# First layer's MLP: plain products replaced by seven half-size products for eight, with the context tokens apart

## The chip, the cores and the metric

One core of one Trainium2 chip runs the whole program. The metric is the device time of one launch in microseconds (us); before the change it is 2879.24 us, the median of 3 runs (2877.9 to 2879.73).

## What is computed

The reference is a two-layer backbone over 1024 latent tokens and 256 context tokens of width 1024. Layer 0 (even) mixes by latent attention and a chunked gate, layer 1 (odd) by gated linear attention. Every layer modulates its RMS norm with vectors that come from the conditioning (six vectors per layer, each a 1024x1024 product with one vector), and closes with a squared-ReLU MLP of hidden width 4096:

```python
def sqrelu_mlp(h, w1, w2):
    return jnp.square(jax.nn.relu(h @ w1)) @ w2

xl = xl + ml[5] * sqrelu_mlp(modulate(rmsnorm(xl, norm2_g[i]), ml[3], ml[4]), mlp_w1[i], mlp_w2[i])
if need_ctx:   # layer 0 only
    xc = xc + mc[5] * sqrelu_mlp(modulate(rmsnorm(xc, norm2_g[i]), mc[3], mc[4]), mlp_w1[i], mlp_w2[i])
```

So layer 0's MLP serves 1280 tokens, layer 1's only the 1024 latent ones. Everything is float32.

## The kernel before, in words

**Products.** Tokens lie along the free dimension in three parts, `TCS`: latent 0 (512), latent 1 (512) and context (256), called 0, 1 and 2 here as in the code. TensorE multiplies float32 by splitting each operand into a rounded part and the rest ("hi" and "lo"): `mm3` (lines 204 to 206) issues hi·hi, hi·lo and lo·hi, three matmuls for one 128x128 weight block and one part of tokens. The hi of a weight is a cast on ScalarE (line 165), its lo a subtraction on VectorE (line 171). A weight block of 1024 columns is loaded through the pool `raws` (3 buffers) and split by `load_w`; `Weights.take(depth)` hands out the next one and first fills the queue up to `depth` blocks ahead. Almost all other tiles share the pool `slots`, 43 buffers of 4 KB per partition.

**Layer 0's MLP** is `mlp` (lines 1096 to 1170). For each of 16 pairs of hidden blocks it takes two blocks of w1, multiplies them with the parts in the order `O3`, makes relu squared and its split, takes two blocks of w2, multiplies and adds into x at once (line 1154). The first pair goes through `first_gemm`, which applies the norm chunk by chunk. Beside it, the generator `bg` makes layer 1's modulation vectors with `ada`: for each of 48 weight tiles of 512 KB a dot product with the conditioning, for the first 16 tiles also with the context's vector. One dot product is a multiplication on GpSimd and a summing activation on ScalarE (`ada_dot`, lines 318 and 319), the other one multiply-and-sum on VectorE (`ada_reduce`, line 332).

**Layer 1's MLP** is `FastMlp` (lines 1173 to 1673). It treats the two latent halves and the halves of the weights as a 2x2 product and needs seven half-size products for eight (the steps A11, A12, S2, S1, S3, S4, A22 of `STEPS`). Its right operands (names 11, 21, 22 and T1 to T4, four tiles each) come from the modulated norm by `scaled`, `shifted`, `half` and `combine`. In `first` (lines 1476 to 1515) one step is 12 matmuls of 512 columns; a pair of hidden blocks has seven steps. Around the products, each step prepares a weight operand three steps ahead (`prepare`: cast on ScalarE, subtraction on VectorE), and `took` handles the result of the step before. A `Hidden` that is "light" squares with two activations on ScalarE (lines 1297, 1298); one that is not does it on VectorE (line 1302). The first two pairs (`PLAIN`) of layer 1 are plain, the next two (`EARLY`) partly, the other 12 take all seven steps. The second product runs over 28 jobs of four groups of 12 matmuls each.

**What sets the order.** Outside `FastMlp.run` a scheduler orders each engine's instructions by the order of their emission and by what is ready. Inside `FastMlp.run` (`manual_schedule`, lines 1570 to 1576) each of the five queues takes its instructions strictly in the order in which the code emits them, so an instruction that waits holds all behind it on its engine. `half` emits, for one chunk,

```python
self.scaled(0, k)                                   # VectorE, line 1210
nc.scalar.activation(hi, t, AF.Identity, bias=b)    # ScalarE, line 1217
nc.vector.scalar_tensor_tensor(lo, t, b, f(hi), op0=ALU.add, op1=ALU.subtract)   # VectorE, line 1218
```

and `apply_norm` (lines 273 to 288) the same three with lines 276, 277, 280. `combine` and `prepare` go through `FastMlp.split`, which emits the cast, then the pending subtraction of the call before. `Norm.begin` is four small matmuls, a VectorE step, a power on GpSimd and a VectorE step (lines 233 to 237); `Norm.end` is a matmul (line 246).

**Around it.** `out_proj` before the MLP ends with the blocks of its last two output chunks part by part in the order `O3`, and begins and ends the norm of a part behind the blocks of the next. `odd_proj` after it starts with `first_gemm` on two weight blocks.

## Time and profile before

| | |
|---|---|
| median of 3 runs | 2879.24 us (2877.9 to 2879.73) |
| profiled execution's own time | 2879.53 us |
| its span, first to last instruction | 2877.7 us |
| TensorE busy | 2755.9 us (96%), mean granted clock 0.983 |
| VectorE, ScalarE, GpSimd busy | 1945.6, 1221.7 and 668.0 us |
| first matmul to last of layer 0's MLP | 780.3 to 1675.2 us |

Times in views are microseconds from the span's start unless marked ns. Matmuls are pipelined: the duration of one is longer than the distance between the starts of two, and the work of a stretch is counted with that distance. PE is TensorE, PEld its weight load, DVE VectorE, ACT ScalarE, POOL GpSimd, SP SyncE. A wait is put down to the engine whose signal came last.

### The profile page before, as it was taken

What the parts mean: (1) busy time and instruction counts of PE and PEld (TensorE: products, weight loads), DVE (VectorE), ACT (ScalarE), POOL (GpSimd) and SP (SyncE); (2) the same over time, 40 slices, a digit from 0 to 9 for tenths busy, and PEclk for the clock granted to TensorE, in tenths of its full rate; (3) what the DMA queues carried; (4) which work ended last, traced back from release to release, by engine and by line L of the source; (5) the groups of instructions that cost most, each with busy time, mean ns of one, the idle gap of its engine ahead of it and who ended that gap; (6) DMA issues with size and microseconds to landing.
All of it is one profiled execution on the core that took longest, in us unless ns stands there. A gap on an engine that the chain in (4) does not pass through costs nothing.

```text
span 2877.7 us, 38606 instructions
## 1 busy us (share of the span) xinstructions
PE 2755.9 (96%) x14752; PEld 2364.8 (82%) x14752; DVE 1945.6 (68%) x3271; ACT 1221.7 (42%) x2375; POOL 668.0 (23%) x608
## 2 busy tenths in 40 slices
PE   5999999999799999999999999999899999999997
PEld 3887899888688888888888878997788788888885
DVE  7848788886778745544544571544774867788887
ACT  4534677774333233222212241876452533344342
POOL 4335455532432332210000010114620111100000
PEclk9999999999899999999999999999999999999998
DMA  6232000026223232321111121335254444483431
GB/s 242 70 115 71 13 13 17 15 88 214 81 74 95 96 103 88 96 73 37 51 31 37 54 74 52 110 112 182 102 198 146 182 159 143 160 302 138 154 135 64
DMA packets 109914, 301.11 MB, mean 105 GB/s; under 512 B 10816, under 2 KB 24256, under 8 KB 109728
## 3 DMA queue, kind: packets, MB, share of 16 engines
q1 hardware_dynamic: 93232, 242.00, 24.9%
q0 software_dynamic: 16496, 56.63, 5.4%
q8 instruction: 116, 1.90, 0.3%
q14 instruction: 70, 0.57, 0.1%
HBM read 229.39 MB, written 69.21 MB: 104 GB/s over the span
## 4 chain that ended last, share of the span: by engine, by line
PE 76%; DVE 9%; issue 6%; ACT 3%; POOL 3%; DMA 3%; SPq 0%; POOLq 0%; DVEq 0%; ACTq 0%
PE b L204 22%; PE b L206 22%; PE b L205 22%; PE b L883 2%; PE b L868 2%; DVE adaj L332 1%; PE b L458 1%; POOL adaj L318 1%; DVE wlo L171 1%; DMA ada<-in_adaT 1%; PE b L1819 1%; DVE h L280 1%; DVE acc L225 1%; DMA hr<-hsp 1%; PE b L1775 1%
## 5 line engine op out<-in xcount | busy, mean ns | idle before, releaser
L204 PE MATMUL b<-h,whi 128*128 128x512 f32 (+1 forms) x1544 | 563.3, 367 | 3.7 <-ACT h L277 1.8
L206 PE MATMUL b<-h,wlo 128*128 128x512 f32 (+1 forms) x1544 | 560.7, 363 | 4.9 <-DVE wlo L171 4.8
L205 PE MATMUL b<-h,whi 128*128 128x512 f32 (+1 forms) x1544 | 561.8, 364 | 3.4 <-DVE h L280 2.2
L205 PEld LDWEIGHTS b<-h,whi 128*128 128x128 f32 x1544 | 294.0, 190 | 52.0 <-DVE h L171 3.2
L206 PEld LDWEIGHTS b<-h,wlo 128*128 128x128 f32 x1544 | 293.6, 190 | 52.0 <-DVE wlo L171 6.9
L204 PEld LDWEIGHTS b<-h,whi 128*128 128x128 f32 x1544 | 293.3, 190 | 51.2 <-ACT h L165 3.2
L205 PE MATMUL b<-B,W 128*128 128x512 f32 (+1 forms) x840 | 325.8, 388 | 5.6 <-DVE B L1566 5.6
L204 PE MATMUL b<-B,W 128*128 128x512 f32 (+1 forms) x840 | 325.9, 388 | 3.6 <-DVE u L1331 3.1
L1154 DVE SCALAR_TENSOR_TENSOR x<-b,mod,x 128x512 f32<-128x512 f32 (+1 forms) x384 | 248.5, 659 | 117.4 <-PE b L206 115.1
L206 PE MATMUL b<-B,W 128*128 128x512 f32 (+1 forms) x840 | 325.2, 387 | 0.0
L318 POOL TENSOR_TENSOR adaj<-ada,sc 128x1024 f32<-128x1024 f32 x80 | 220.6, 2774 | 381.4 <-PE b L206 184.3
L204 PE MATMUL b<-hid,whi 128*128 128x512 f32 (+1 forms) x768 | 272.8, 355 | 0.0
L205 PE MATMUL b<-hid,whi 128*128 128x512 f32 (+1 forms) x768 | 272.0, 354 | 0.0
L206 PE MATMUL b<-hid,wlo 128*128 128x512 f32 (+1 forms) x768 | 271.9, 354 | 0.0
L1123 DVE TENSOR_TENSOR relu<-relu 128x512 f32<-128x512 f32 (+1 forms) x96 | 79.6, 835 | 193.8 <-ACT relu L1116 193.8
L319 ACT ACTIVATE adaj<-adaj 128x1024 f32<-128x1024 f32 x80 | 84.8, 1061 | 294.0 <-POOL adaj L318 294.0
L205 PEld LDWEIGHTS b<-B,W 128*128 128x128 f32 x840 | 159.3, 190 | 39.6 <-DVE B L1566 7.7
L204 PEld LDWEIGHTS b<-B,W 128*128 128x128 f32 x840 | 159.3, 190 | 36.9 <-ACT W L165 3.1
L206 PEld LDWEIGHTS b<-B,W 128*128 128x128 f32 x840 | 159.2, 189 | 31.2
L171 DVE TENSOR_TENSOR wlo<-raw,whi 128x1024 fp32r<-128x1024 f32 x120 | 153.0, 1281 | 45.2 <-ACT whi L165 43.6
L204 PEld LDWEIGHTS b<-hid,whi 128*128 128x128 f32 x768 | 145.5, 189 | 20.5 <-issue 0.2
L205 PEld LDWEIGHTS b<-hid,whi 128*128 128x128 f32 x768 | 145.4, 189 | 20.3 <-issue 0.2
(288 smaller groups left out, 5690.9 us busy)
## 6 DMA issues: line engine op xcount, KB each, us to landing
raw<-in_w SPq DMA_DIRECT2D x130, 512.0 KB, 4.2
ada<-in_adaT SPq DMA_DIRECT2D x96, 512.0 KB, 4.2
hr<-hsp SPq DMA_DIRECT2D x56, 512.0 KB, 4.1
hsp<-hid POOLq DMA_DIRECT2D x48, 512.0 KB, 4.8
raw<-in_od_win SPq DMA_DIRECT2D x25, 512.0 KB, 3.7
x<-in_xT SPq DMA_DIRECT2D x20, 512.0 KB, 8.4
xsp<-x SPq DMA_DIRECT2D x16, 512.0 KB, 3.8
x<-xsp SPq DMA_DIRECT2D x16, 512.0 KB, 10.4
```

What stands on the lines that cost most here:

```text
L171: (lo or nc.vector).tensor_sub(dst[1], src, f(dst[0]))
L204: nc.tensor.matmul(ps, lhsT=ah, rhs=bh, start=start, stop=False, skip_group_check=more)
L205: nc.tensor.matmul(ps, lhsT=ah, rhs=bl, start=False, stop=False, skip_group_check=more)
L206: nc.tensor.matmul(ps, lhsT=al, rhs=bh, start=False, stop=stop, skip_group_check=more)
L225: (add or nc.vector).tensor_add(acc, acc, sq)
L280: nc.vector.scalar_tensor_tensor(dst[1], t, b[:, d:d + 1], f(dst[0]), op0=ALU.add, op1=ALU.subtract)
L318: nc.gpsimd.tensor_mul(j, t, sc[w])
L319: nc.scalar.activation(j, j, AF.Copy, accum_out=mod(l, part, w)[:, d:d + 1])
L868: nc.tensor.transpose(tb[:, a, b], p[:, o:o + P], ident)
L883: nc.tensor.matmul(av, lhsT=V[self.kts[2 * g + a]][:, h], rhs=self.pts[g][:, a, s], start=(g == 0 and a == 0 and s == 0), stop=(g == ng - ...
L1123: nc.vector.tensor_mul(r, r, r)
L1154: nc.vector.scalar_tensor_tensor(x, ps, gate[i][:, d:d + 1], x, op0=ALU.mult, op1=ALU.add)
```

## The change

Layer 0's MLP is made by `FastMlp` as well, now with all 16 pairs taking seven steps (`plain` and `early` are 0), all light. The context tokens don't fit into that scheme: `context_in` multiplies them with all 32 blocks of w1 in front and stores the hidden values in memory, `context_out` multiplies these with all of w2 behind; both load and split the weights a second time for it. `context_in` makes the right operands of the latent products beside its blocks, two steps of `operands` per block; `context_out` begins the next layer's norm and applies it for the latent parts. Layer 1's modulation vectors are made by `ada_paced`, both dot products on VectorE, one tile at every odd step of `first`, the tile loaded two steps ahead into `raws`. `O3` puts the context first. Layer 1's own MLP keeps its parameters.

```diff
+    csp = dr.tile([NFF, P, 256], F32, name="csp", tag="csp")
+    cxsp = dr.tile([ND, P, 256], F32, name="cxsp", tag="cxsp")
...
+    def load_halves(src):
+        raw = raws.tile([P, 2, 512], F32, name=nm("raw"), tag="raw")
+        nc.sync.dma_start(raw, src.rearrange("b p c -> p b c"))
+        return split_w(raw.rearrange("p b c -> p (b c)"))
...
+    def ada_paced(items):
+        for l, part, which in items:
+            for d in range(ND):
+                t = raws.tile([P, D], F32, name=nm("ada"), tag="raw")
+                nc.sync.dma_start(t, adaT[l, part * ND + d])
+                yield
+                for w in which:
+                    j = t if w == which[-1] else slot([D], n="adaj")
+                    nc.vector.tensor_tensor_reduce(j, t, sc[w], scale=1.0, scalar=0.0, op0=ALU.mult, op1=ALU.add,
+                                                   accum_out=mod(l, part, w)[:, d:d + 1])
+                t = None
+            for w in which:
+                ada_end(l, part, w)
...
                     elif pace:
-                        while (0, k) not in on_chip:
+                        while (order[0], k) not in on_chip:
                             run(load, 1)
...
-    def mlp(l, norm, order, gate, bg, ab, parts=None, done=None):
...
-        def __init__(self, l):
-            self.l = l
+        def __init__(self, l, plain, early, bg=iter(())):
+            self.l, self.plain, self.early, self.bg = l, plain, early, bg
...
-            nc.gpsimd.dma_start(bsp[k], f(self.made_last))
+            if self.plain:
+                nc.gpsimd.dma_start(bsp[k], f(self.made_last))
...
-            early = p < EARLY
+            early = p < self.early
-                self.hids[p] = self.Hidden(p, early)
+                self.hids[p] = self.Hidden(p, early or not self.early)
...
             NP = self.NP
-            steps = [(p, c) for p in range(PLAIN, NP) for c, _, _ in STEPS
-                     if p >= EARLY or c in ("S1", "S2", "S3", "S4", "A22")]
+            steps = [(p, c) for p in range(self.plain, NP) for c, _, _ in STEPS
+                     if p >= self.early or c in ("S1", "S2", "S3", "S4", "A22")]
             todo, n = [], 0
-            for p in range(PLAIN, NP):
+            for p in range(self.plain, NP):
                 mine = [c for q, c in steps if q == p]
-                if p == EARLY:
+                if p == self.early and p:
                     for c in ("11", "21"):
                         todo.append((n - 7, lambda c=c: self.again(c)))
-                if p > PLAIN:
+                if p == 0:
+                    todo += [(k - 3.5, lambda c=c: self.prepare(0, c)) for k, c in enumerate(mine) if k > 2]
+                elif p > self.plain:
                     todo.append((n - 8, lambda p=p: self.load_pair(p)))
...
+            self.late = None
...
                 self.product(held[o], self.ops.pop((p, c)), b, new)
+                if n % 2:
+                    run(self.bg, 1)
                 if last:
...
-        def run(self, gate, parts, done):
+        def run(self, *args):
-            out = self.all(gate, parts, done)
+            out = self.all(*args)
-        def all(self, gate, parts, done):
+        def operands(self):
+            for k in range(8):
+                self.half(k)
+                yield
+            self.spill(0)
+            for j in range(4):
+                self.scaled(1, j)
+                self.scaled(1, j + 4)
+                yield
+                self.shifted("22", j + 4)
+                self.combine("T1", j)
+                yield
+            self.spill(1)
+            self.norm.xs = self.xs = None
+            for c in ("T2", "T3", "T4"):
+                for j in range(4):
+                    self.combine(c, j)
+                    if c == "T3":
+                        del self.ts[1, j]
+                    yield
+            self.load_pair(0)
+            yield
+            self.flush()
+            for c in ("S1", "S2", "S3", "S4"):
+                self.add_up(0, c)
+                yield
+            for c in ("A11", "A12", "S2"):
+                self.prepare(0, c)
+                yield
+        def context_in(self):
+            norm = self.norm
+            self.late, self.T = None, {}
+            for j, t in enumerate(norm.xs[2].tiles):
+                nc.sync.dma_start(cxsp[4 * j:4 * j + 4].rearrange("d p t -> p d t"), t)
+            self.xs = norm.xs
+            b = norm.ab[0][1]
+            self.db = small(4, n="db")
+            nc.vector.tensor_sub(self.db, b[:, 4:8], b[:, 0:4])
+            ops = self.operands()
+            late = None
+            def act(b, ps):
+                r = tmp([256], n="r")
+                nc.scalar.activation(r, ps, AF.Relu)
+                if b % 4 == 0:
+                    self.c = slot([4, 256], n="hc")
+                nc.scalar.activation(self.c[:, b % 4], r, AF.Square)
+                if b % 4 == 3:
+                    nc.gpsimd.dma_start(csp[b - 3:b + 1].rearrange("b p t -> p b t"), self.c)
+                    self.c = None
+            for b in range(NFF):
+                w = W.take(min(2, NFF - 1 - b))
+                ps = bank([512])[:, :256]
+                gemm(ps, w, norm.hs[2])
+                w = None
+                if b < 2:
+                    (norm.end if b else norm.begin)(1)
+                run(ops, 2)
+                if late:
+                    late()
+                late = lambda b=b, ps=ps: act(b, ps)
+            run(ops)
+            late()
+            self.flush()
+            norm.hs[2] = None
+        def context_out(self, gate, after, x):
+            after.xs[2] = x
+            self.c = self.t = None
+            def fetch(b):
+                t = slot([4, 256], n="hc")
+                nc.sync.dma_start(t, csp[b:b + 4].rearrange("b p t -> p b t"))
+                return t
+            def made(b):
+                if b % 4 == 0:
+                    self.t = self.u
+                if b % 4 == 2:
+                    self.u = fetch((b + 2) % NFF)
+                if b % 2 == 0:
+                    self.c = slot([2, 2, 256], F32R, n="B")
+                o = self.c[:, b % 2, 0], self.c[:, b % 2, 1]
+                split(o, self.t[:, b % 4])
+                return o
+            self.u = fetch(0)
+            h = made(0)
+            n = 0
+            for m in range(2):
+                pss = [bank([512])[:, :256] for _ in range(4)]
+                for b in range(NFF):
+                    if b % 2 == 0:
+                        w = W.take(min(2, (NFF - 2 - b) // 2 + (1 - m) * NFF // 2))
+                    cs = (b % 2) * 512
+                    for g in range(4):
+                        ds = slice(cs + g * P, cs + (g + 1) * P)
+                        mm3(pss[g], (w[0][:, ds], w[1][:, ds]), h, b == 0, b == NFF - 1)
+                    if n in (2, 4, 6, 8):
+                        (after.end if n % 4 == 0 else after.begin)((n - 2) // 4)
+                    if b % 2:
+                        w = None
+                    n += 1
+                    if n < 2 * NFF:
+                        h = made(b + 1 if b + 1 < NFF else 0)
+                    if n >= 10 and n % 4 == 0:
+                        for i in range(2):
+                            after.apply(i, min((n - 8) // 4, ND))
+                for g in range(4):
+                    d = 4 * m + g
+                    nc.vector.scalar_tensor_tensor(x[d], pss[g], gate[2][:, d:d + 1], x[d], op0=ALU.mult, op1=ALU.add)
+                    after.accs[2] = sumsq(after.accs[2], x[d], 256)
+            self.c = self.t = self.u = None
+            return after
+        def all(self, gate, parts, done, ab=None):
-            self.begin()
+            if self.plain:
+                self.begin()
+            else:
+                self.context_in()
...
-            accs = [None] * len(parts)
-            after = Norm([[x[:, q[1]:q[2]] for x in xs[q[0]]] for q in parts], accs,
-                         [(0, q[2] - q[1]) for q in parts], self.norm.ab)
+            if self.plain:
+                accs = [None] * len(parts)
+                after = Norm([[x[:, q[1]:q[2]] for x in xs[q[0]]] for q in parts], accs,
+                             [(0, q[2] - q[1]) for q in parts], self.norm.ab)
+            else:
+                accs = [None] * 3
+                after = Norm(xs + [None], accs, TCS, ab)
...
-                cuts = [(0, 256), (256, 512)] if last else [(0, 512)]
+                cuts = [(0, 256), (256, 512)] if last and done else [(0, 512)]
...
-                        if last:
+                        if last and done:
...
+            if not self.plain:
+                self.context_out(gate, after, load_x(cxsp, 0, 256))
...
-    O3, O2 = (0, 2, 1), (0, 1)
+    O3, O2 = (2, 0, 1), (0, 1)
-    ff = lambda l: [lambda l=l, c=c, j=j, w=w: load_w(w[l, c * 2 + j])
-                    for c in range(NFF // 2) for w in (w1, w2) for j in range(2)]
-    W.add(*[lambda d=d: load_w(ev_wout[d]) for d in range(ND)], *ff(0))
+    W.add(*[lambda d=d: load_w(ev_wout[d]) for d in range(ND)])
+    W.add(*[lambda b=b: load_w(w1[0, b]) for b in range(NFF)])
+    W.add(*[lambda b=b, m=m: load_halves(w2[0, b:b + 2, :, m * 512:m * 512 + 512])
+            for m in range(2) for b in range(0, NFF, 2)])
...
-    bg = chain(*(ada(1, p, (0, 1) if p < 2 else (0,)) for p in range(6)))
-    norm = mlp(0, norm, O3, both(0, 5), bg, mods2(1, 0))
-    pre = odd_proj(norm, O3)
+    fast = FastMlp(0, 0, 0, ada_paced([(1, p, (0, 1) if p < 2 else (0,)) for p in range(6)]))
+    fast.norm = norm
+    norm = fast.run(both(0, 5), [(0, 0, 512), (1, 0, 512)], None, mods2(1, 0))
+    pre = odd_proj(norm, (0, 1, 2))
-    fast = FastMlp(1)
+    fast = FastMlp(1, PLAIN, EARLY)
```

## Rows read from the trace of the kernel before

**Rows 1.** The page's first part: busy time, share of the span, instructions.
```profile
PE 2755.9 (96%) x14752; PEld 2364.8 (82%) x14752; DVE 1945.6 (68%) x3271; ACT 1221.7 (42%) x2375; POOL 668.0 (23%) x608
```

**Rows 2.** Windows: stretch, its length, busy time by engine (instructions), clock, DMA share, GB/s.
```profile
780.30:1675.20 894.90, 889.55 (x4634) 766.03 (x4633) 522.55 (x743) 239.74 (x399) 147.89 (x61) 1.00 0.22 70
1675.20:1700.00 24.80, 23.02 (x125) 19.05 (x124) 23.10 (x43) 13.15 (x24) 4.29 (x3) 1.00 0.18 64
2321.00:2521.00 200.00, 200.00 (x884) 165.62 (x883) 148.66 (x232) 62.32 (x115) 27.23 (x40) 1.00 0.43 152
2560.00:2790.00 230.00, 229.84 (x1014) 190.02 (x1013) 195.07 (x306) 95.90 (x173) 0.00 (x0) 1.00 0.43 153
```

**Rows 3.** Timeline of PE, layer 0's MLP: 23 matmuls of 512 columns, 24 of 256.
```profile
899.78 0.39 PE L205 MATMUL b<-h,whi 128*128 128x512 f32 x1
...
904.99 0.28 PE L204 MATMUL b<-h,whi 128*128 128x256 f32 x1
...
907.87 0.40 PE L204 MATMUL b<-h,whi 128*128 128x512 f32 x1
```

**Rows 4.** Timeline of ACT and DVE, layer 1: weight split, then four `scaled`.
```profile
2238.97 1.03 ACT L165 CAST whi<-raw 128x1024 fp32r<-128x1024 f32 x1
2240.03 1.23 DVE L171 TENSOR_TENSOR wlo<-raw,whi 128x1024 fp32r<-128x1024 f32 x1 [0.23 <-ACT whi L165]
2241.17 2.72 DVE L1210 SCALAR_TENSOR_TENSOR t<-x,mod,b 128x512 f32<-128x512 f32 x4
```

**Rows 5.** The same view: hi of one chunk; cast and lo of one `combine`.
```profile
2207.58 0.72 ACT L1217 ACTIVATE B<-t,mod 128x512 fp32r<-128x512 f32 x1 [0.70 <-DVE t L1210]
...
2247.18 0.62 ACT L165 CAST B<-T 128x512 fp32r<-128x512 f32 x1 [1.38 <-DVE T L1244]
2247.83 0.69 DVE L1190 TENSOR_TENSOR B<-T,B 128x512 fp32r<-128x512 f32 x1 [0.69 <-ACT B L165]
```

**Rows 6.** Groups by line: engine, operation, count, busy us, mean ns, idle before.
```profile
L165 ACT CAST hid<-relu 128x256 fp32r<-128x256 f32 x32 | 12.8, 404 | 11.0 <-DVE relu L1123 11.0
L171 DVE TENSOR_TENSOR hid<-relu,hid 128x256 fp32r<-128x256 f32 x32 | 13.4, 421 | 9.0 <-ACT hid L165 9.0
```

**Rows 7.** Timeline of DVE: a norm's begin, with the power on POOL between its two steps.
```profile
2188.04 0.16 DVE L235 TENSOR_SCALAR rs<-b 128x4 f32<-128x4 f32 x1
...
2189.32 0.69 DVE L237 TENSOR_TENSOR acc<-ident,rs 128x512 f32<-128x512 f32 x1 [1.05 <-POOL rs L236]
```

**Rows 8.** Timeline of DVE and ACT, layer 1, pair 3, which is light: one square.
```profile
2308.12 0.68 DVE L1294 TENSOR_TENSOR c<-b,u 128x512 f32<-128x512 f32 x1
2310.67 0.69 DVE L1190 TENSOR_TENSOR W<-S,W 128x512 fp32r<-128x512 f32 x1 [1.87 <-ACT W L165]
...
2308.84 0.63 ACT L1297 ACTIVATE c<-c 128x512 f32<-128x512 f32 x1 [1.36 <-DVE c L1294]
...
2310.04 0.60 ACT L165 CAST W<-S 128x512 fp32r<-128x512 f32 x1
```

**Rows 9.** Multiply-and-sum on DVE: one beside quiet POOL, then the group over all.
```profile
755.52 1.21 DVE L332 CUSTOM_DVE_ANT_0 adaj<-ada,sc 128x1024 f32<-128x1024 f32 x1
...
L332 DVE CUSTOM_DVE_ANT_0 adaj<-ada,sc 128x1024 f32<-128x1024 f32 x76 | 132.9, 1766 | 11.7 <-DMA ada<-in_adaT 11.6
```

**Rows 10.** Timeline of PE: end of `out_proj`, then the second product's first job in layer 1.
```profile
760.63 1.86 PE L233 MATMUL b<-ones,acc 128*128 128x1 f32 x8 [16.70 <-DVE acc L225]
766.99 0.41 PE L204 MATMUL b<-h,whi 128*128 128x256 f32 x1
767.20 0.41 PE L205 MATMUL b<-h,whi 128*128 128x256 f32 x1
...
2543.04 0.50 PE L205 MATMUL b<-B,W 128*128 128x512 f32 x1 [1.12 <-DVE B L1566]
```

**Rows 11.** Windows behind that wait; columns as in rows 2.
```profile
760.00:770.00 10.00, 9.37 (x40) 8.51 (x41) 3.07 (x7) 0.83 (x2) 1.04 (x1) 0.59 0.23 79
770.00:780.00 10.00, 10.00 (x48) 8.28 (x47) 5.53 (x10) 3.05 (x5) 0.69 (x1) 1.00 0.00 0
```

71 lines of the change are left out of this document (removed).

## The prediction

> **What bounds the kernel now.** I read the page's shares first: TensorE is busy 96% of the span [rows 1], so time goes only where matmuls go away or where TensorE comes to wait. Then the windows by stage [rows 2]: layer 0's MLP takes 894.9 us and TensorE idles for 5.3 us of it, while layer 1's MLP, already in the seven-product scheme, keeps TensorE as full (200.00 of 200 us in the first product, 229.84 of 230 in the second) with VectorE at 74% and 85%. Then the timeline, for the price of a matmul [rows 3]: 23 of 512 columns start within 5.21 us, 0.2266 us each; 24 of 256 within 2.88 us, 0.120 us each. Last the timelines of VectorE and ScalarE, for the handoffs between the two, since inside `FastMlp.run` every queue is strictly in order.
>
> The faster scheme removes matmuls, but the context's blocks now stand alone at 2.88 us each, and beside them stands work that was spread over 894.9 us. The question is how long that work takes in order.
>
> **Matmuls removed.** Before, per part: 32 blocks x 8 chunks x 3, for w1 and for w2, 1536 matmuls; 1536 x (2 x 0.2266 + 0.120) = 880.5 us. After: latent 16 pairs x 7 steps x 12 and 28 jobs x 48, 2 x 1344 x 0.2266 = 609.1; context 1536 x 0.120 = 184.3, together 793.4. Gain 87.1 us. The stage before has 894.9 - 880.5 = 14.4 us beyond its matmuls (idle, norm matmuls, a low clock at its start), and `odd_proj` idles 1.8 us at its start [rows 2]. All this goes; below stands what comes instead.
>
> **Context in front.** One block in program order: cast of the weight two blocks ahead, its subtraction, the 24 matmuls, two steps of `operands`, relu and square of the block before. ScalarE's next cast stands behind that square, and VectorE's next subtraction behind that cast, so the two engines form one chain per block, and TensorE gets weights at its pace. Prices [rows 4]: cast 1.03, then the subtraction, whose successor starts 1.14 later; four `scaled` take 2.72, so 0.66 from start to start and 0.74 alone; a hi 0.72, a cast of 512 0.62 and a subtraction 0.69 [rows 5], which with the same overlap of 0.08 costs 0.60 to 0.61 where the next is ready; relu and square of 256 some 0.4 each, like the cast of that shape [rows 6].
> - Blocks 1 to 3 hold two `half` each, and in `half` VectorE waits for ScalarE's hi before its lo: 1.05 + 1.14 + (0.75 + 0.72 + 0.66) + (0.75 + 0.66) + 0.7 + handoffs of 0.03 = 6.6 us. Block 0 has `norm.begin` instead of a relu: TensorE's 2.9, four small matmuls, 1.28 to the step behind the power [rows 7], then two halves, 9.1 us.
> - Blocks 4 to 7 (two `scaled`, a hi, a lo, T1): 1.05 + 1.14 + 0.66 + 0.75 + 0.72 + 0.66 + 0.68 + 0.53 + 0.7 + handoffs = 7.0 us.
> - Blocks 8 to 13 (two of T2 to T4, subtraction deferred): 1.05 + 1.14 + 0.66 + 0.60 + 0.75 + 0.53 + 0.7 = 5.5 us.
>
> Sum 9.1 + 19.8 + 28 + 33 = 89.9; 2.2 later block 16 has its weights, and 16 more blocks at 2.88 make 138.2 us against 92.2 of matmuls: **+46**. Lower bound, if the handoffs were hidden: VectorE alone has 1.14 + 2.4 per block, 18 blocks x 0.65 = +11; upper bound +56, if buffers of `slots` run short and each of the 14 blocks pays 0.7 us more for a subtraction. I take the chain, as the queues are in order and rows 5 show VectorE idle for such a cast.
>
> **First product.** Per pair VectorE has seven subtractions, four sums, four differences and three additions, 18 x 0.605 = 10.9 us of 19.03. Being light, each of three squares puts two activations and a cast between an addition and the next subtraction: 1.87 us of waiting [rows 8]; one of the three lies under the sums. 14.7 us, no bound. Now 64 multiply-and-sums come in, two per odd step for the first 16 tiles, one for 32 more. The trace has one at 1.21 us beside a quiet GpSimd, as long as a weight's subtraction, so a successor comes 1.14 later [rows 4]; the mean of all is 1.77 [rows 9]. GpSimd only issues stores here, so 1.14: 2 x 3.5 x 1.14 = 8.0 make 22.7 us per pair, 3.7 over TensorE's, for 32 steps or 4.57 pairs: 17; minus one step's slack at A22 (2.7): **+14.5**. With one per odd step 18.7 us, just covered. Bounds: +5 (the waits overlap) and +60 (price 1.77, below). Between the products TensorE waits 1.1 in layer 1 [rows 10]: **+1.1**.
>
> **Context behind.** Its start: the last residual add, a square, the cast of h and of the first weight (nothing is fetched ahead) and its subtraction, some 4 us, and 1.5 more until the second h: +5.5. Two begins at 2.4 us each of subtraction, power and the lo of the next h, which is made only one block ahead: +4.8, and 2.4 for the norms' matmuls. Then eight times per four blocks (5.76 us) two `apply_norm`, each waiting for its hi: 2 x 2.16, two weight subtractions 2.28, four of 256 some 1.4, and 0.4 until the weight's cast: 8.4 us. 8 x 2.65 less 3 to 4 of lead: +17.5. **+30** in all; bounds +10 and +40. **`odd_proj`** has no weights ready now: two casts and subtractions behind the last squares, **+6**; bounds 1 and 9.
>
> **`out_proj`.** Context first: its last blocks are shorter cover, its norm is cheaper. The wait of 16.70 us for the sum of squares [rows 10] moves with VectorE's backlog and isn't removed. 0; bounds -8 and +5. Modulation off GpSimd and ScalarE: no gain, both have slack; 48 loads of 512 KB on SyncE, 25 MB in 305 us, hide beside 16 MB of weights: 134 GB/s, where layer 1's first product moved 152 without a wait [rows 2]. Each takes the one buffer of `raws` that two pairs of weights leave, and its wait for the release holds the next pair's loads on SyncE's queue; these are due three steps (8.2 us) before they are used, so I add nothing, and a late landing is inside the +60. Stores of context and x: hidden.
>
> **Sum.** -87.1 - 14.4 - 1.8 + 46 + 14.5 + 1.1 + 30 + 6 = -5.7 us. Against the profiled execution's own 2879.53 (span 2877.7, median 2879.24): **2874 us**. The matmul gain is nearly all given back. 0.2% (5.8 us) is about what a measurement of this kernel can tell from no change, so the forecast sits on that edge: 2858 to 2890 with the terms' small errors.
>
> **Clock.** Behind the 16.70 us wait [rows 10] the granted clock is 0.59, partly the lower of the two levels (1.2 and 2.4 GHz), and 1.00 in the ten us after [rows 11]; a matmul of 256 then starts every 0.21 us [rows 10], a block 5.1 us. In front, TensorE idles half of each block, so it may sit at the lower level. That is still below the chain's 5.5 to 7.0 us and costs nothing until block 14; I add nothing.
> The Trainium skill (TensorE: Matmul & The Clock Gate, section "HAM oscillation — how this bites in real kernels") says that waits between bursts put the array back to the lower clock every time, which speaks against blocks apart. The trace agrees that a wait lowers it and shows a quick return.
>
> **Rivals.**
> - *Handoffs hidden, most of the gain kept.* VectorE's load alone decides: +11, +5, +10 in place of 46, 14.5, 30: 64.5 us less, 2809. For it: rows 2 show layer 1's same code without stalls. Against it: there a block of TensorE is 5.4 us or more, here 2.88 and 1.44. Something between, 2809 to 2858, is likeliest of it. 0.30.
> - *Slower: the multiply-and-sum at 1.77 us.* In `first`, VectorE at rows 9's mean would need 14.7 + 12.4 = 27.1 us per pair for 4.57 pairs and 20.9 for 11.4: 37 + 21 = 58 instead of 14.5, 2917. It decides above about 1.3 us per sum, where the -5.7 and 5.8 more are gone. For it: 76 of them average that. Against it: those ran beside GpSimd's own multiplications, gone here. With shares of it, 2890 to 2917. 0.20.
> - *Clock stays low.* If the lower level held through the last 16 context blocks, 16 x 2.25 = 36 us more: 2910. Rows 11 speak against it. 0.06. By that rule of the Trainium skill (TensorE: Matmul & The Clock Gate) the whole context part would run so, and this would be its time.
>
> **Chances.** Forecast case 0.44 (faster 0.20, same 0.17, slower 0.07), the others 0.30, 0.20, 0.06: faster 0.50, same 0.17, slower 0.33. The range leaves out a tenth at each end: 2828 to 2908; the forecast's own is 2858 to 2890.
>
> **What would show it.** Right: in the first 90 us of the stage TensorE about half busy, waiting for weight subtractions behind hi's casts; a context stage of some 138 us; waits at A22 in the first 85 us of the first product, none later; behind, stalls in eight clusters at `apply_norm`. Wrong: a context stage near 105 us (gain kept), or VectorE full through all of the first product with multiply-and-sums above 1.3 us (slower).

## The result and the profile after

The change made the kernel slower. Its median is 2905.14 us (4 runs, 2901.53 to 2911.41) against 2879.48 us for the kernel before on the same chip (4 runs): the ratio is 1.0089, with a 95% interval of 1.0068 to 1.0110. The forecast was 2874 us, faster by 0.2%: the range held the time, the direction was wrong. The profiled execution of the changed kernel took 2901.53 us, with a span of 2899.8 us.

Busy time, share of the span and instructions of each engine in the changed kernel, to be set beside [rows 1]:

```profile
PE 2720.6 (94%) x14368; PEld 2327.0 (80%) x14368; DVE 2092.8 (72%) x3591; ACT 1406.0 (48%) x2739; POOL 567.1 (20%) x621
```

The windows of the four stages that stand where [rows 2] has one MLP of 894.9 us (stretch, its length, busy time of PE, PEld, DVE, ACT and POOL, granted clock, DMA share, GB/s): context in front, first product, second product, context behind.

```profile
777.01:926.46 149.45, 119.97 (x780) 111.49 (x779) 85.72 (x109) 73.41 (x128) 6.39 (x8) 0.87 0.50 162
926.46:1256.16 329.70, 314.62 (x1347) 255.73 (x1346) 254.67 (x423) 162.84 (x293) 41.26 (x61) 0.98 0.66 227
1256.16:1568.77 312.61, 307.96 (x1345) 252.75 (x1343) 261.51 (x410) 130.91 (x233) 2.70 (x4) 0.99 0.47 168
1568.77:1702.47 133.70, 112.16 (x790) 107.25 (x789) 90.64 (x144) 68.19 (x121) 4.44 (x3) 0.89 0.65 201
```

Against the prediction, in us:

| stretch | before | predicted | after | missed by |
|---|---|---|---|---|
| up to the end of `out_proj` | 780.3 | 780.3 | 777.0 | -3.3 |
| context in front | | 138.2 | 149.5 | +11.3 |
| first product | | 319.1 | 329.7 | +10.6 |
| second product | | 305.7 | 312.6 | +7.0 |
| context behind | | 122.2 | 133.7 | +11.5 |
| from `odd_proj` on | 1202.5 | 1206.7 | 1197.3 | -9.4 |
| span | 2877.7 | 2872.0 | 2899.8 | +27.8 |

That the range held the time owes something to luck: the four stages missed by 40.4 us together, and 12.7 us came back before and behind them, for reasons outside the sum.

The four stages now take 925.5 us where the one took 894.9. TensorE's waits in them, summed from the list of who waited for whom, by stretch in the order of the stages:

```profile
PE b L212 <- ACT whi L167: 14.5, 12, 1.6
PE b L214 <- DVE wlo L173: 12.9, 17, 0.8
PE b L213 <- DVE h L288: 1.1, 2, 0.9
PE b L212 <- ACT h L285: 0.8, 2, 0.5
...
PE b L212 <- ACT u L1280: 15.0, 9, 3.9
...
PE b L213 <- DVE B L1518: 4.5, 4, 2.3
...
PE b L213 <- DVE B L173: 9.9, 9, 2.2
PE b L212 <- ACT B L167: 7.7, 5, 3.7
PE b L212 <- ACT whi L167: 2.8, 1, 2.8
PE b L214 <- DVE wlo L173: 0.7, 1, 0.7
PE b L212 <- DVE x L1645: 0.4, 1, 0.4
```

Beyond their matmuls at full pitch (92.2, 304.6, 304.6 and 92.2) the stages lose 57.3, 25.1, 8.1 and 41.5 us. The waits are 29.3, 15.0, 4.5 and 21.5 of it. What is left, 28.0, 10.1, 3.6 and 20.0 us, stands behind waits: by the starts of matmul after matmul in the timeline some 19, 7, 2 and 13 us of it are matmuls at the lower clock, and most of the rest is the restart, about 0.3 us behind each wait. So nearly half of the loss is no wait but what follows one. Not all of it could be had back alone. Where the two engines' chain sets the pace, as in the first 95 us of the front, a faster matmul would only wait longer; the cycles there came out as worked out from the two engines' work alone. The timeline of TensorE behind the first long wait of the first product shows how (start us, length us):

```profile
956.18 0.39 PE L214 MATMUL b<-B,W 128*128 128x512 f32 x1
960.28 0.50 PE L212 MATMUL b<-B,W 128*128 128x512 f32 x1 [3.71 <-ACT u L1280]
...
961.95 0.63 PE L214 MATMUL b<-B,W 128*128 128x512 f32 x1
962.38 0.63 PE L212 MATMUL b<-B,W 128*128 128x512 f32 x1
...
964.96 0.40 PE L213 MATMUL b<-B,W 128*128 128x512 f32 x1
965.20 0.40 PE L214 MATMUL b<-B,W 128*128 128x512 f32 x1
```

From 961.10 to 964.09 us a matmul of 512 columns starts every 0.43 us instead of every 0.23, the lower of the two clock levels, and then the pitch is back. The wait of 3.71 us cost 1.8 us more. The same stands behind the other three waits of 2.2 us and more in this product, and behind none of its five of 1.34 us and less. Over both products of this kernel and of all versions below, but for the one with GpSimd's products, every wait of 3.49 us and more brings 1.7 to 3.1 us, no wait of 2.00 us or less brings more than the restart, and of 18 waits of 2.23 to 2.33 us fifteen bring 1.7 to 2.9 us and three only 0.3. Where waits follow each other within a few us the clock falls with shorter ones: in the front's chain, with none above 1.65 us, it is 0.81 (796.00 to 875.00 us).

### The profile page after: what moved, and what is told of

Its sections match the earlier page's. It is cut to its first block, busy times and chain, and to the rows that moved or that the text cites. A ratio compares the mean times of both kernels' runs of the same rounds, so it can differ in the third digit from the quotient of the medians.

```text
span 2899.8 us, 39070 instructions
## 1 busy us (share of the span) xinstructions
PE 2720.6 (94%) x14368; PEld 2327.0 (80%) x14368; DVE 2092.8 (72%) x3591; ACT 1406.0 (48%) x2739; POOL 567.1 (20%) x621
## 4 chain that ended last, share of the span: by engine, by line
PE 59%; DVE 16%; issue 11%; ACT 8%; DMA 4%; POOL 3%; SPq 0%; POOLq 0%; DVEq 0%; ACTq 0%
PE b L212 17%; PE b L213 17%; PE b L214 17%; PE b L906 2%; PE b L891 2%; DMA ada<-in_adaT 2%; DVE ada L362 1%; DVE W L1136 1%; PE b L481 1%; DVE hid L1252 1%; DVE wlo L173 1%; POOL adaj L326 1%; DVE c L1241 1%; ACT c L1244 1%; DVE adaj L340 1%
## 5 line engine op out<-in xcount | busy, mean ns | idle before, releaser
L212 PE MATMUL b<-B,W 128*128 128x512 f32 (+1 forms) x1736 | 679.0, 391 | 19.1 <-ACT u L1280 15.0
L213 PE MATMUL b<-B,W 128*128 128x512 f32 (+1 forms) x1736 | 678.4, 391 | 10.1 <-DVE B L1518 9.9
L214 PE MATMUL b<-B,W 128*128 128x512 f32 (+1 forms) x1736 | 676.8, 390 | 0.0
L212 PEld LDWEIGHTS b<-B,W 128*128 128x128 f32 x1736 | 329.1, 190 | 92.8 <-ACT u L1280 19.7
L213 PEld LDWEIGHTS b<-B,W 128*128 128x128 f32 x1736 | 329.5, 190 | 81.7 <-DVE B L1518 14.7
L212 PE MATMUL b<-h,whi 128*128 128x512 f32 (+1 forms) x1032 | 377.1, 366 | 17.9 <-ACT whi L167 14.5
L214 PE MATMUL b<-h,wlo 128*128 128x512 f32 (+1 forms) x1032 | 372.3, 361 | 18.7 <-DVE wlo L173 18.6
L214 PEld LDWEIGHTS b<-B,W 128*128 128x128 f32 x1736 | 329.3, 190 | 66.9
L213 PE MATMUL b<-h,whi 128*128 128x512 f32 (+1 forms) x1032 | 370.9, 360 | 2.7 <-DVE h L173 1.5
L167 ACT CAST W<-raw 128x512 fp32r<-128x512 f32 x310 | 191.6, 619 | 264.4 <-DVE raw L1483 104.4
L212 PEld LDWEIGHTS b<-h,whi 128*128 128x128 f32 x1032 | 206.0, 200 | 48.8 <-ACT whi L167 17.3
L213 PEld LDWEIGHTS b<-h,whi 128*128 128x128 f32 x1032 | 206.7, 200 | 30.6 <-DVE h L173 2.8
L167 ACT CAST B<-hr 128x512 fp32r<-128x512 f32 x224 | 138.3, 617 | 55.9 <-PE b L214 40.8
L1518 DVE TENSOR_TENSOR B<-hr,B 128x512 fp32r<-128x512 f32 x224 | 153.9, 687 | 6.1 <-ACT B L167 6.1
L1518 DVE TENSOR_TENSOR W<-raw,W 128x512 fp32r<-128x512 f32 x224 | 153.5, 685 | 0.8 <-ACT W L167 0.6
L212 PE MATMUL b<-whi,h 128*128 128x256 f32 (+1 forms) x500 | 145.2, 290 | 0.0
```

Of the source, the lines that this page charges most:

```text
L167: eng.copy(dst, src)
L212: nc.tensor.matmul(ps, lhsT=ah, rhs=bh, start=start, stop=False, skip_group_check=more)
L213: nc.tensor.matmul(ps, lhsT=ah, rhs=bl, start=False, stop=False, skip_group_check=more)
L214: nc.tensor.matmul(ps, lhsT=al, rhs=bh, start=False, stop=stop, skip_group_check=more)
L1518: nc.vector.tensor_sub(lo, a, f(hi))
```

## The experiments

All times of a stage are of one profiled execution of each kernel (331.6, 149.4 and 133.5 us in the expectations are other readings of the stages given above as 329.7, 149.5 and 133.7); the ratios are against the kernel before on the same chip, with their 95% intervals.

**First product: sums, loads or clock.** VectorE and ScalarE of the changed kernel ahead of that wait of 3.71 us:

```profile
954.21 0.69 DVE L1136 TENSOR_TENSOR W<-S,W 128x512 fp32r<-128x512 f32 x1
954.81 1.22 DVE L362 CUSTOM_DVE_ANT_0 adaj<-ada,sc 128x1024 f32<-128x1024 f32 x1
956.08 1.23 DVE L362 CUSTOM_DVE_ANT_0 ada<-ada,sc 128x1024 f32<-128x1024 f32 x1
957.23 0.69 DVE L1241 TENSOR_TENSOR c<-b,s 128x512 f32<-128x512 f32 x1
...
957.95 0.63 ACT L1244 ACTIVATE c<-c 128x512 f32<-128x512 f32 x1 [7.85 <-DVE c L1241]
959.65 0.58 ACT L1280 COPY u<-b 128x512 f32<-128x512 f32 x1
```

The two sums stand ahead of A12's addition (957.23), ScalarE's square waits for that addition, and the copy of S2 (959.65), which frees the bank that S3's matmuls need, stands behind the square on ScalarE's queue. The first run takes the sums away and keeps the loads:

```diff
-  nc.vector.tensor_tensor_reduce(j, t, sc[w], ..., accum_out=mod(l, part, w)[:, d:d + 1])
+  nc.vector.tensor_copy(mod(l, part, w)[:, d:d + 1], t[:, 0:1])
```

> Leaves out the modulation's multiply-and-sums of layer 1 that the first product carries: each becomes a copy of one column, so the output is not the reference's; the loads stay. After has a first product of 331.6 us where its matmuls are 304.6, with 15.0 us of waits for ScalarE's copy in its first 140 us and a granted clock of 0.95 there. Theory (VectorE's sums, two per odd step, stand ahead of an addition that a square on ScalarE needs, and the clock falls after each such wait): the waits and the low clock both go, the first product takes 305 to 310 us, the time falls by 20 to 27 us to about 2880. Rival 1 (the loads of the modulation, 25 MB beside the weights, hold TensorE): nothing changes, within 5 us of 2905. Rival 2 (only the waits belong to the sums, the low clock comes from the start of the stage): 15 us less, the clock stays at 0.95 in the first 130 us.

Measured: 2877.05 us, ratio 1.0000 (0.9988 to 1.0012). The window of its first product:

```profile
923.72:1228.39 304.67, 304.67 (x1346) 252.26 (x1345) 187.15 (x359) 166.63 (x293) 41.26 (x61) 1.00 0.70 242
```

No wait is left and the clock is 1.00: 25.0 us are gone where the waits were 15.0. Both rivals fall. The lower clock came with the waits, and the loads, now 242 GB/s, hold nobody.

The second run keeps the sums, and spreads them:

```diff
-  if n % 2:
+  if (n * 66) // 112 > ((n - 1) * 66) // 112:   # and one sum per issue
       run(self.bg, 1)
```

> The same sums, spread evenly: one at a time, in 66 of the first 112 steps, in place of two per odd step for 32 steps and one for the next 32. Theory (it is the double rate of the first 85 us that delays VectorE, not the sums as such): VectorE then needs about 10.9 us of its own, 1.9 of waits and 0.59 x 7 x 1.14 = 4.7 us of sums per pair of 19.0 us, so no wait for ScalarE's copy is left, the first product takes about 307 us, the time falls by 20 to 25 us to 2880 to 2885. Rival 1 (the sum itself is too dear wherever it stands): the waits spread over the product and their total stays at 15 us. Rival 2 (loads): no change.

Measured: 2899.97 us, ratio 1.0075 (1.0060 to 1.0090); first product 325.0 us, 15 waits for ScalarE's copy, 12.9 us in all. A miss: the total of the waits hardly moved, as the first rival says. The double rate was not the cause by itself. The run without sums shows why: in the steps after A12 VectorE has no idle time at all, in others it idles 1.9 us for ScalarE. So it is the place of a sum that counts, which the third run tries:

```diff
+  if n % 7 in (0, 4, 5, 6):
+      run(self.bg, 1)
   self.product(held[o], self.ops.pop((p, c)), b, new)
-  if n % 2:
-      run(self.bg, 1)
```

> The same sums, one at a time, but only in the four steps of a pair (S1, S3, S4, A22) in which the run without sums shows VectorE idle ahead of a weight's subtraction (0.60, 1.96, 1.87 and 1.87 us, for ScalarE's rounding behind a square), and each ahead of that subtraction. Theory (a sum costs TensorE nothing where VectorE would idle in any case, and its whole 1.2 us where it stands ahead of the steps after A12, in which VectorE is full): waits below 2 us in all, the granted clock stays at 1.00, the first product takes 305 to 308 us, the time falls by 20 to 25 us to about 2881. Rival (the sum is too dear wherever it stands, as the even spread left 12.9 us of waits): waits of 10 us or more remain and the first product takes 318 us or more.

Measured: 2897.11 us, ratio 1.0057 (1.0039 to 1.0074); first product 318.2 us. Of the waits for ScalarE 1.1 us are left, but a new one of 8.6 us has come, at its end. VectorE's and TensorE's timelines there:

```profile
1242.66 1.23 DVE L364 CUSTOM_DVE_ANT_0 ada<-ada,sc 128x1024 f32<-128x1024 f32 x1 [10.78 <-DMA ada<-in_adaT]
...
1244.56 0.79 PE L212 MATMUL b<-B,W 128*128 128x512 f32 x1 [8.63 <-DVE c L1243]
```

Four sums a pair last until the product's end, and there the load of a modulation tile stands on SyncE's queue behind eight loads for the second product. From 1215 to 1245 us the DMA engines are also busy throughout (390 GB/s), so how much of the delay is the place in the queue and how much the traffic is not shown. The theory holds for the sums in the gaps, and missed this load.

The fourth run undoes the modulation's part alone: products on GpSimd, sums on ScalarE.

```diff
-  nc.vector.tensor_tensor_reduce(j, t, sc[w], ...)
+  if owed:
+      owed.pop()()
+  nc.gpsimd.tensor_mul(j, t, sc[w])
+  owed.append(...)          # nc.scalar.activation(j, j, AF.Copy, accum_out=...)
```

> Undoes the modulation's part of the change alone: each product on GpSimd (2.59 us in the kernel before) and its sum on ScalarE one issue later (1.06 and 0.18 us), 64 of them at the evenly spread places where VectorE's own sums left a first product of 325.0 us with 12.9 us of waits. Theory (VectorE's in-order queue, full in the steps after A12, is what the sums hold up): without them there VectorE is on time, ScalarE has 1.24 us more per sum but is half idle, so a first product of 305 to 310 us, time about 2882, as in the run that leaves the sums out. Rival (GpSimd's products slow VectorE beside them, as the 1.77 us mean of its sums against 1.21 alone in the kernel before says): 166 us of GpSimd's time cost VectorE some 0.8 us per product, waits of 8 us or more remain, a first product of 318 us or more.

Measured: 3004.64 us, ratio 1.0431 (1.0413 to 1.0448); first product 427.9 us. The rival, far above its own bound. VectorE beside three products of GpSimd:

```profile
1008.16 8.41 DVE L1145 TENSOR_TENSOR W<-S,W 128x512 fp32r<-128x512 f32 x1
...
1008.96 7.05 POOL L368 TENSOR_TENSOR adaj<-ada,sc 128x1024 f32<-128x1024 f32 x3
```

A subtraction that takes 0.69 us elsewhere took 8.41 and ended 0.6 us after the third product. The Trainium skill (SBUF — State Buffer, section "SBUF: two separate sides") says that VectorE's operations with two inputs in SBUF and GpSimd's that read SBUF exclude each other, one of them waiting for the whole instruction of the other. The trace agrees, and goes further: VectorE stayed out over three products in a row. In this first product VectorE's additions with one operand in PSUM kept their 0.68 to 0.69 us in the mean, while W<-S,W, with both in SBUF, took 1.45 instead of 0.69. At the same places VectorE's own sums gave 325.0 us, so the move to VectorE was not the mistake.

**Context in front.** The order of VectorE's instructions in a block is changed, nothing else:

```diff
 def shifted(self, c, k):
-    nc.vector.scalar_tensor_tensor(lo, t, b, f(hi), ...)
+    self.flush()
+    self.low = low            # that instruction, held back until the next operand
 # context_in, per block
+    W.lows = []               # load_w puts its subtraction here
     w = W.take(min(2, NFF - 1 - b))
     ...
     run(ops, 2)
+    for low in W.lows:
+        low()
```

> In the 16 blocks that carry operands, the weight's low part is issued on VectorE behind the block's operands, and a half's low part is held back until the next operand is made, so that neither stands waiting for ScalarE's rounding. The same instructions, another order. After has 149.4 us for the context in front, with cycles of 6.5, 7.0 and 5.5 us from one weight's rounding to the next. Theory (each cycle is one chain through two in-order queues): cycles of about 3.8, 4.3 and 3.7 us, where each engine's own work is left, and a context in front of 110 to 115 us; the time falls by 30 to 38 us to about 2870. Rival 1 (the load of weights paces it, 16 MB in 95 us): cycles stay above 5 us, less than 10 us gained. Rival 2 (the low clock paces it, 0.66 to 0.84 there): a block at 24 x 0.21 = 5.1 us is the floor, cycles stop at 5.1 and the front is about 135 us; 14 us gained.

Measured: 2877.50 us, ratio 0.9993 (0.9983 to 1.0002); context in front 119.8 us instead of 149.5. ScalarE's weight casts in the changed kernel (one cycle each of halves, T1, and T2 to T4), then TensorE's waits in this run:

```profile
797.70 1.03 ACT L167 CAST whi<-raw 128x1024 fp32r<-128x1024 f32 x1
804.23 1.03 ACT L167 CAST whi<-raw 128x1024 fp32r<-128x1024 f32 x1
...
817.79 1.03 ACT L167 CAST whi<-raw 128x1024 fp32r<-128x1024 f32 x1
824.83 1.03 ACT L167 CAST whi<-raw 128x1024 fp32r<-128x1024 f32 x1
...
850.07 1.03 ACT L167 CAST whi<-raw 128x1024 fp32r<-128x1024 f32 x1
855.63 1.03 ACT L167 CAST whi<-raw 128x1024 fp32r<-128x1024 f32 x1
```

```profile
800.77 0.38 PE L220 MATMUL b<-h,wlo 128*128 128x256 f32 x1 [0.65 <-DVE wlo L186]
804.55 0.39 PE L220 MATMUL b<-h,wlo 128*128 128x256 f32 x1 [0.65 <-DVE wlo L186]
...
817.56 0.39 PE L220 MATMUL b<-h,wlo 128*128 128x256 f32 x1 [1.18 <-DVE wlo L186]
821.88 0.39 PE L220 MATMUL b<-h,wlo 128*128 128x256 f32 x1 [1.18 <-DVE wlo L186]
825.54 0.39 PE L220 MATMUL b<-h,wlo 128*128 128x256 f32 x1 [0.54 <-DVE wlo L186]
```

Cycles of 6.53, 7.04 and 5.56 us became 3.78, 4.32 and 3.66. Both rivals fall: the loads of the weights keep up with 3.7 us, and with short waits the clock stays high (0.97 over the stage, 0.87 before). The stage is 5 us above what was expected; the first three blocks still take 16 us.

**Context behind.** Three runs: two changes, each alone on the changed kernel, then both together. First both rounded parts of a pair of norms ahead of both low parts:

```diff
-  for i in range(2):
-      after.apply(i, min((n - 8) // 4, ND))
+  lows = [norm_hi(after.xs[i][d], after.y[i], after.ab[i], d, after.hs[i][d], 512) for i in range(2)]
+  for low in lows:
+      low()
```

> In the context behind, the two halves' norms of x give both their rounded parts first and then both low parts, in place of one after the other. After has 133.5 us for that stage, with clusters of 8.4 us per four blocks. Theory (VectorE waits in each of eight clusters, twice, for ScalarE's rounding): the second rounding lies beside the second half's own work, about 1.2 us less per cluster, a cycle of about 7.2 us, the stage 8 to 10 us shorter, time about 2896. Rival (the wait for the raw weights, 17 us in all on ScalarE's queue, sets the cycle): no change beyond 3 us.

Measured: 2902.37 us, ratio 1.0081 (1.0066 to 1.0097); the stage took 122.1 us, 11.6 less, and a cluster's cycle fell from 8.36 (VectorE's first norm at 1599.61, the next at 1607.96) to 6.8 us (1617.80, then 1624.62). The stage shows the theory right. The whole moved by 3 us only: other stretches of that execution are longer (`out_proj` ends at 784.2, and from `odd_proj` on it takes 1201.4), and the four runs lie 10 us apart.

Then, on the changed kernel, fetching ahead:

```diff
-  h = made(b + 1 if b + 1 < NFF else 0)     # one block ahead
+  hq.pop(0)
+  more(1)                                   # four blocks ahead
 # beside the last job of the second product
+  W.fill(1); W.fill(2); more(2); more(2)    # spread over its four output chunks
```

> Context behind: its first two weights and first four operands are made beside the last job of the second product, and the operands stay four blocks ahead instead of one; the norms' order is unchanged. After takes 133.5 us there: waits of 2.8, 0.7, 2.2, 2.2 us in the first 30 us and of 3.7 and 0.7 at the half, and a granted clock of 0.66 to 0.83 for 30 us. Theory (the waits are few, but the clock falls behind each and the blocks then take 5.0 us instead of 2.9): without these 12 us of waits the clock stays at 1.00 and the stage loses 12 us of waits and some 12 more of low clock; VectorE's clusters of 8.4 us per four blocks stay, so about 112 us, time about 2884. Rival 1 (the clock is low there whatever the waits, as short matmuls of 256 columns draw it down): the waits go, the clock stays below 0.85 in the first 30 us, the stage at 122 us or more. Rival 2 (the loads of the weights pace the start, 4.4 us of ScalarE's waiting): the start shrinks by less than 5 us.

Measured: 2895.62 us, ratio 1.0057 (1.0038 to 1.0076); the stage took 121.3 us. The windows of the first 30 us, of the changed kernel and of this run:

```profile
1571.74:1602.00 30.26, 25.18 (x137) 23.13 (x138) 16.43 (x27) 11.36 (x20) 2.04 (x2) 0.72 0.67 209
```

```profile
1571.29:1602.00 30.71, 29.15 (x229) 27.59 (x228) 23.84 (x39) 16.78 (x31) 2.04 (x2) 1.00 0.80 271
```

229 matmuls in place of 137 in 30 us, at a clock of 1.00: the same short matmuls, without the waits. So the clock was low for the waits, and the first rival falls in its reason. But a number near its 122 is what came. The waits fell only from 21.5 to 16.9 us, since the clusters kept theirs and at the half 5.6 us (for VectorE's residual step, L1655) came in place of 4.4; what stands behind waits fell from 20.0 to 12.2. The expectation left out the half.

Both together, with a pair of norms every six blocks:

```diff
-  if n >= 10 and n % 4 == 0:
+  if n >= 10 and n % 6 == 0:
```

> Context behind: both rounded parts before both low parts, a pair of norms every six blocks instead of every four, and operands and weights fetched ahead as above. Per six blocks TensorE needs 8.64 us, VectorE three weight subtractions, six of 256 and four of 512, about 8.8. Theory (VectorE's work between two clusters against TensorE's sets the stage): no wait beyond 0.3 us is left in the clusters, the stage takes 94 to 99 us against 92.2 of matmuls, time about 2868. Rival (the low clock stays whatever the waits): 108 us or more.

Measured: 2879.13 us, ratio 0.9998 (0.9988 to 1.0009); the stage:

```profile
1573.11:1674.01 100.90, 97.31 (x790) 95.05 (x788) 87.72 (x141) 64.44 (x116) 2.04 (x2) 1.00 0.79 261
```

100.9 us for 92.2 of matmuls, 3.6 of it waits, at full clock: 2 us above the theory's 94 to 99, far below the rival's 108. Waits of 0.59 and 0.78 us are left in the clusters, where the theory had none beyond 0.3. The whole fell by 26 us and not by 37: from `odd_proj` on this execution takes 1204.0 us for the changed kernel's 1197.3, 1.9 us of it a wait for a norm's sum at the start of `odd_proj`, which the changed kernel does not have. In the six versions with a changed context behind this part takes 1200.7 to 1204.0 us, in the six without 1197.3 to 1200.4, so some of the gain is given back there.

**All of it.** The front reordered, sums in the gaps, the behind as in the last run, and in the second product the addition to the sum of squares placed behind the next low parts:

> All of it: the front reordered, the sums in the gaps, the behind as just described, and in the second product the addition to the sum of squares placed behind the next low parts. Theory (the losses are separate places on TensorE's path, so they add up): 29.7 us from the front, 22 to 25 from the first product, 35 to 39 from behind, 2 to 3 from the second product's end, 2905 - 91 = about 2814, some 2.2% below the kernel before. Rival (what one stage gains, the next gives back, since VectorE's and the loads' backlog only moves on): less than 60 us gained, 2845 or more.

Measured: 2833.82 us, ratio 0.9838 (0.9821 to 0.9854). 71 us are gained on the changed kernel: the stages' gains nearly add up (28.3, 11.0, 5.3 and 27.2 us), and what is missing from 91 is the late modulation load (first product 318.7) and a wait of 2.6 us early in the context behind. SyncE's queue there holds stores of x, which wait for the last residual steps, ahead of operands and weights:

```profile
1513.71 7.81 SPq L2044 DMA_DIRECT2D xsp<-x  x2
1521.62 0.41 SPq L1624 DMA_DIRECT2D hc<-csp  x1
1522.08 1.56 SPq L193 DMA_DIRECT2D raw<-in_w  x2
```

The next run moves these stores, and tries a way out of the late load:

```diff
-  nc.sync.dma_start(t, adaT[l, part * ND + d])
+  nc.gpsimd.dma_start(t, adaT[l, part * ND + d])
-      run(self.bg, 1)
+      run(self.bg, 2 if n % 21 == 12 else 1)
 # odd_proj: stores of x
-  nc.sync.dma_start(xsp[...], t)
+  nc.gpsimd.dma_start(xsp[...], t)
```

> All the repairs together, and three more that their traces ask for: the modulation's loads on GpSimd's queue instead of SyncE's, where the last ones stood behind eight loads of the second product's weights (10.8 us of VectorE's waiting, 8.4 us of TensorE's); five sums earlier, so that none is left at the end; and the stores of x on GpSimd's queue, which on SyncE's stood waiting for the last residual adds ahead of the weights of the context behind. Theory (what is left of the first product's 318.7 us above its 304.6 is the late load and the low clock behind it, and of the context behind's 106.3 us the 2.6 us wait and 10 us at a clock of 0.64 behind it): first product 306 to 309, behind 97 to 101, time 2815 to 2820. Rival 1 (the loads are late because the DMA engines are full, at 300 GB/s and above there, whatever the queue): less than 5 us gained, 2830 or more. Rival 2 (GpSimd's stores of the hidden parts wait for VectorE and hold the modulation's loads in their turn): waits for these loads spread over the product, 320 us or more there.

Measured: 2843.77 us, ratio 0.9871 (0.9854 to 0.9887). The stores' part worked (context behind 99.8 us at a clock of 1.00); the loads' part gave rival 2's number: first product 326.4 us, VectorE waiting 45.2 us for modulation tiles, up to 3.5 us each. Some of these loads stand behind four stores of hidden parts, which take 2.7 us to issue, and the loads land 5.5 us after their issue in the median, where the next run on SyncE's queue has 4.4. How the delay divides between the two is not shown. The last run puts these loads back on SyncE's queue and issues some sums earlier:

```diff
-      run(self.bg, 2 if n % 21 == 12 else 1)
+      run(self.bg, 2 if n % 7 == 5 and 7 < n < 49 else 1)
```

> The repairs together, with the modulation's loads back on SyncE's queue, six sums of the first two-sum tiles issued as second ones of a step in pairs 1 to 6, so that the last sum stands ahead of the loads of the second product's weights, and the stores of x on GpSimd's queue. Theory (GpSimd's queue held the loads up, since its stores of hidden parts wait for VectorE; on SyncE's queue only the last ones were late): first product 306 to 310 us instead of 318.7 and 326.4, behind 98 to 101, second product 307, time 2815 to 2822. Rival (a tile's load, which is issued only once the sum before it has given its buffer back, is late wherever sums follow each other at 2.7 us, and doubles make it worse): first product 316 us or more, 2826 or more.

Measured: 2817.71 us (5 runs, 2815.66 to 2819.39), ratio 0.9786 (0.9773 to 0.9799). Its windows, in the order of the stages:

```profile
777.08:897.96 120.88, 103.62 (x780) 97.89 (x779) 83.50 (x109) 73.43 (x128) 6.40 (x8) 0.97 0.61 200
897.96:1206.80 308.84, 306.75 (x1346) 251.79 (x1345) 253.71 (x423) 164.89 (x293) 41.37 (x61) 1.00 0.68 242
1206.80:1513.79 306.99, 305.25 (x1346) 252.17 (x1344) 262.08 (x413) 132.52 (x237) 7.73 (x11) 1.00 0.49 174
1513.79:1614.15 100.36, 97.35 (x790) 95.11 (x789) 87.17 (x141) 64.19 (x116) 2.75 (x3) 1.00 0.77 252
```

All four numbers are as expected. 837.1 us in place of 925.5, with the work of the change in another order and the stores of x on another queue: this version beats the kernel before by 2.1%.

## Why the prediction was wrong

- **Matmuls removed and the old overhead:** right. The pitches hold (304.67 us for 1344 matmuls in the run without sums), so 101.5 us were there to be gained.
- **Context in front, +46; it was +57.3.** The chain through two in-order queues was right within 0.1 us: cycles of 6.53, 7.04 and 5.56 us where 6.6, 7.0 and 5.5 were worked out, and the reordered run shows that it was the order and not the work. Missed: the start (the fifteenth weight's cast came 95.2 us after the start where 89.9 were summed) and the last blocks, 54.3 us from that cast where 48.3 were counted, since ScalarE waited for late weight loads (1.22, 2.27, 0.76 and 1.37 us from 874 to 889) and then, ahead of a weight's cast, twice for a store of hidden values to land (3.65 and 3.66 us). TensorE's waits from 872 us on are 5.0 us, about half behind each. The granted clock is 1.00 there. "16 more blocks at 2.88" took the loads for granted, and no term stood for the stores of hidden values. ScalarE at the first of these, then TensorE, then the window of the last blocks:

```profile
899.07 0.42 ACT L1578 ACTIVATE hc<-r 128x256 f32<-128x256 f32 x1 [3.65 <-DMA csp<-hc]
...
900.47 0.39 PE L212 MATMUL b<-h,whi 128*128 128x256 f32 x1 [0.55 <-ACT whi L167]
...
875.00:926.46 51.46, 47.26 (x381) 45.87 (x380) 22.68 (x23) 28.61 (x52) 3.01 (x4) 1.00 0.64 204
```

- **First product, +14.5; it was +25.1.** The waits are 15.0 us, the size predicted, but not by the model predicted: they stand at S3 and not at A22, they come from where the sums stand and not from a pair that is over-full, they go on, smaller, to 1209.76 us, and one sum per step does not hide them (spread evenly: 12.9 us). So the size was luck. The other 10.1 us are some 7 of lower clock, the step "I add nothing" under **Clock**, and restarts.
- **Second product, +1.1; it was +8.1.** The wait at its start came (1.02); two of 0.97 and 2.29 us in the last jobs were not seen: there VectorE adds to a sum of squares, waiting for ScalarE's square, ahead of the next low parts. With that addition moved the product takes 307.0 us.
- **Context behind, +30; it was +41.5.** The begins and the clusters came as described (2.21 and 2.18 us for 2.4 each, a cycle of 8.36 us for 8.4); the start was shorter (2.81 and 0.70 us for 5.5). Not counted were 4.4 us of waits at the half and the lower clock behind the waits, 0.72 from 1571.74 to 1602.00 us.
- **`odd_proj`, +6; it was nothing.** ScalarE's timeline at the end of the stage:

```profile
1695.09 1.06 ACT L167 CAST whi<-raw 128x1024 fp32r<-128x1024 f32 x1 [0.46 <-DMA raw<-in_od_win]
1697.75 1.05 ACT L167 CAST whi<-raw 128x1024 fp32r<-128x1024 f32 x1 [1.60 <-DMA raw<-in_od_win]
1702.11 0.42 ACT L232 ACTIVATE sq<-x 128x256 f32<-128x256 f32 x1 [3.31 <-DVE x L1645]
```

  `odd_proj`'s weights are cast ahead of the last squares, though the code emits them later. The prediction took everything emitted later to stand behind the hand-ordered stage. The stretch is 9.4 us below its forecast; the other 3.4 us are not explained. The stores of x on SyncE's queue are the same effect with the other sign.
- **`out_proj`, 0:** right within what runs differ by; it ended 3.3 us earlier, and between 775.3 and 784.2 in the other executions.
- **Clock.** This is the step that failed. The prediction priced a low clock only where blocks stand alone, saw that the chain hides it there, and added nothing: no term for the stages in which a wait stands among full matmuls. It holds for the front's chain. But the five waits of 2.2 us and more in the two products each brought 1.7 to 2.2 us behind them, and in the context behind the waits brought some 13 us, about 10 of them outside the clusters that VectorE paces. That is some 20 us, reckoned from the starts of matmuls, the largest term that the sum lacks. Without it the span would have been near 2880 us, no clear change from the kernel before; most of what then still parts it from the forecast are the front's 11.3 us and the waits that were not counted. No run takes the low clock away and leaves the waits; the run without sums, where 15.0 us of waits took 10.0 us more with them, comes nearest. That rule of the Trainium skill (TensorE: Matmul & The Clock Gate, section "HAM oscillation — how this bites in real kernels") was weighed as all or nothing, 2910 if the clock stays low. The trace agrees with it in part: low again after each long wait, and back some ten matmuls later.
- **Loads.** The 134 GB/s set against layer 1's 152 leave out the stores, which the 152 hold. The first product moved 227 GB/s, 28 of its 75 MB stores. The loads held nobody in the run without sums; a late one held TensorE at the end of the product where the sums lasted that long.
- **Rivals.** The hidden handoffs fall. What spoke for them was layer 1's "same code" [rows 2], but from 2321 to 2521 us that code squares on VectorE (42 times, line 1302), and here all squares are on ScalarE, where the copy that TensorE waits for stands behind them. With them alone, in the run without sums, no wait is left, so they cost only together with the sums; no run tried squares on VectorE here. The multiply-and-sum at 1.77 us falls too: it is 1.22 us here; its time, 2917, came near for another reason. So did the 2910 of the clock that stays low: in the last context blocks, where it was to be low, it is 1.00.

## What to carry to other kernels

A product scheme that shortens TensorE's blocks is paid for by the handoffs that the longer blocks covered: work out each block's chain through the in-order queues, and before giving the gain up, issue the waiting halves of the handoffs later, which costs no instruction. Put side work where the engine would idle in any case, ahead of an instruction that waits for another engine, and never ahead of one that another engine waits for; an even spread is not that. Price a wait of TensorE at its length and, in a stage that is otherwise full, add the matmuls at the lower clock behind it, as the rows show them (in the two products here mostly some 2 us behind a wait of 2.2 us or more, nothing behind one of 2.0 or less).

## What the runs showed that was not expected

- A VectorE subtraction of two operands in SBUF took 8.41 us instead of 0.69 beside three products of GpSimd in a row; the first product then took 427.9 us instead of 329.7.
- By the prediction's terms a wait costs its length. Removing 15.0 us of waits gave 25.0 us, and removing waits at the start of the context behind brought 229 matmuls of 256 columns into 30 us where 137 had been.
- Loads moved to GpSimd's queue, where nothing but stores stood, came later than on SyncE's: VectorE's waiting for them was 45.2 us there and 28.2 us in the last run.
